# One state update for both heads in a chunked linear-attention recurrence, with third load buffers, an ordered weight preparation and scratch tensors split per 512 tokens

## Chip, cores and metric

The kernel runs on one core of one Trainium2 chip. The metric is device time in microseconds (us) of one execution; times before are the median of three runs, and the profile is one further execution.

## What is computed

One layer mixes 2048 tokens of width 1024 in float32. After a modulated RMS norm, one large projection gives the inputs of three mixers: two gated linear attentions (four heads each, key width 64, value width 128 in the first, "GLA", and 64 in the second, "HGRN") and a stick-breaking attention. Their outputs are normalised, gated, multiplied by an output matrix, added to the input and normalised again. The change touches the two gated linear attentions. Cut to what matters, they are, per chunk of 64 tokens:

```python
def step(state, inp):
    q_c, k_c, v_c, g_c = inp
    b_cum = jnp.cumsum(g_c, axis=2)
    ...
    scores = jnp.einsum('bhtd,bhsd,bhtsd->bhts', q_c, k_c, decay)
    o_c = (jnp.einsum('bhts,bhsv->bhtv', scores, v_c)
           + jnp.einsum('bhtd,bhdv->bhtv', q_c * jnp.exp(b_cum), state))
    b_last = b_cum[:, :, -1:, :]
    state = (jnp.exp(b_last[:, :, 0, :, None]) * state
             + jnp.einsum('bhsd,bhsv->bhdv', k_c * jnp.exp(b_last - b_cum), v_c))
    return state, o_c
```

## The kernel before, in words

The program has four stretches in time. First the norm, the modulation and the projections (to about 442 us in the trace), which also compute the decay sums of every chunk (`decay_sums`, L523 to L537) and store decays, queries, keys, values and gates in scratch tensors in device memory. Then the stick-breaking attention (`sb_stream`, to 854 us) with the rest of the projections beside it. Then the recurrence (to 1054 us), beside which the projection of the output gates fills TensorE. Last `phase2`: the outputs of 512 tokens are gathered with their gates, normalised and multiplied by the output matrix, four groups of 512 in turn.

The recurrence works on pairs of heads: two pairs of GLA, then two pairs of HGRN, and for each pair four tiles of 512 tokens (8 chunks), so 16 tiles, numbered 0 to 15 here. `gla_fast` (L879) loads for each tile decays `bc`, queries `qt` and keys `kt`, 128 x 512 each with one head in rows 0 to 63 and the other in rows 64 to 127 (L889 to L891, two buffers each), and `load_values` (L810) loads the values twice: as `Vn` in token order and, chunk by chunk, into `W[h]`.

`W[h]`, one tile per head, holds in 64 of its 128 rows the values of a chunk and in the other 64 the state before that chunk. `M[:, h]` matches it: masked scores in the rows of the values, decayed queries in the rows of the state (the queries' rows change sides for that, L911, one instruction per head). So one product of 128 rows per chunk and head gives the output `o` (L872). Because state rows lie on the other side from their keys, the decay of a chunk is also kept in a side-swapped copy `SX` (L533).

`gla_tail` (L830) goes in three steps: transposes of the keys (L838) and their copy `KTt` by ScalarE (L840); the products `U` of keys and values (L849) and the state updates on VectorE, one per chunk and head (L860):

```python
nc.vector.scalar_tensor_tensor(dst, W[h][orow, n, :], dec[orow, n:n + 1],
                               U[n % 2][orow, n // 2, :],
                               op0=ALU.mult, op1=ALU.add)
```

and the output products with their copies and stores (L872 to L877). `U`, `o`, the transposes and the scores `scp` (L919) have one buffer each in PSUM.

TensorE's order is written out by hand (the loop at L1062): scores and transposes of tile i, three steps of the gate projection (9 products of 512 columns), `U` of tile i, three more such steps, output products of tile i-1. The orders of VectorE, ScalarE, GpSimd and of the DMA queue on SyncE (SP) are set by a planner that simulates the program: an engine takes what its simulation has ready, and each engine then works strictly in that order. `scale_wo` (L1014) prepares one half of the output matrix in four steps from tile 8 of the program on: a load `wr` of 512 KB on SP, a product with the gate on GpSimd, a rounded copy `wh` and the rest `wl` on VectorE. Its `wr` shares two buffers with the gate projection's weight loads `wraw` (L140).

In scratch memory each of `s_gate`, `s_o` and the features is one tensor of 128 x 2048 (L58 to L67). `phase2` starts with tokens 0 to 511 (`prep(0)`): it loads `ot` from `s_o` and `gt` from `s_gate` on SP (L1125, L1129), multiplies them on VectorE and sums squares on TensorE. The gates of those tokens are computed in the second stretch, those of tokens 1024 to 2047 beside the recurrence.

Of the kernel before, what the change touches and what calls it, by code (L numbers as in the profile page):

```python
# [8 lines left out]
F32 = mybir.dt.float32  # L9
# [4 lines left out]
ALU = mybir.AluOpType  # L14
# [4 lines left out]
P = 128  # L19
T = 2048  # L20
# [22 lines left out]
def hybrid_mixer_kernel(ctx, tc, x, c, w_ada, b_ada, w_in, w2, bg, gnw, lbl, hnw,  # L43
# [10 lines left out]
    def act_tables(name):  # L54
# [39 lines left out]
    SE = const.tile([P, 4, T // GTF, 3 * NBF], F32, name="SE")  # L94
    SX = const.tile([P, 4, T // GTF, NBF], F32, name="SX")
    ada_b = const.tile([P, 16], F32, name="ada_b")
# [712 lines left out]

    def load_values(pools, pr, g, GT, Wn):  # L810
# [17 lines left out]
        return Vn, W, new_w() if g + 1 < T // GT else None  # L828

    def gla_tail(gr_, pp, pr, g, GT, M, kd, dec, Vn, W, Wn):  # L830
        gla = pr < 2
# [13 lines left out]
        for n in range(NB):  # L845
            rs = slice((n % 2) * 64, (n % 2) * 64 + 64)
            for h in range(2):
                orow = slice((1 - h) * 64, (1 - h) * 64 + 64)
                mm(U[n % 2][orow, n // 2, :], KTt[rs, n // 2, h * 64:(h + 1) * 64],  # L849
                   Vn[rs, n // 2, h * dv:(h + 1) * dv], start=True, stop=True)  # L850
        for n in range(NB):
            for h in range(2):
                orow = slice((1 - h) * 64, (1 - h) * 64 + 64)
                if n + 1 < NB:
                    dst = W[h][orow, n + 1, :]
                elif Wn is not None:
                    dst = Wn[h][orow, 0, :]
                else:
                    continue
                nc.vector.scalar_tensor_tensor(dst, W[h][orow, n, :], dec[orow, n:n + 1],  # L860
                                               U[n % 2][orow, n // 2, :],
                                               op0=ALU.mult, op1=ALU.add)
        yield


        no = 2 if gla else 1
        o = pp.tile([P, no, GT], F32, tag="o", name="o")
        for n in range(NB):
            ns = slice(n * CB, (n + 1) * CB)
            for h in range(2):  # L870
                dst = o[:, h, ns] if gla else o[h * 64:(h + 1) * 64, 0, ns]
                mm(dst, W[h][:, n, :], M[:, h, ns], start=True, stop=True)  # L872
        for a in range(no):
# [5 lines left out]
    def gla_fast(pairs, gp, gr_, pp, scp):  # L879

        for pr in pairs:
            gla = pr < 2
            j = pr % 2
            s = 1.0 / 16.0 if gla else 1.0
            Wn = None
            for g in range(T // GTF):
                tsl = slice(g * GTF, (g + 1) * GTF)
                bc, qt, kt = (gp.tile([P, GTF], F32, tag=t, name=t) for t in ("bc", "qt", "kt"))
                nc.sync.dma_start(bc, s_feat["da" if gla else "db"][j][:, tsl])  # L889
                nc.sync.dma_start(qt, s_feat["qa" if gla else "qb"][j][:, tsl])  # L890
                nc.sync.dma_start(kt, s_feat["ka" if gla else "kb"][j][:, tsl])  # L891
                Vn, W, Wn = load_values(gr_, pr, g, GTF, Wn)
# [16 lines left out]
                nc.gpsimd.tensor_tensor(v3(kd), v3(eN), per_chunk(2), op=ALU.mult)  # L909
                for h in range(2):  # L910
# [13 lines left out]
                for h in range(2):  # L924
                    hs = slice(h * 64, (h + 1) * 64)
                    nc.gpsimd.affine_select(v3(M[hs, h, :]), v3(S[hs]),
                                            pattern=[[0, NBF], [1, CB]], base=0,
                                            channel_multiplier=-1, compare_op=ALU.is_ge, fill=0.0)
                yield gla_tail(gr_, pp, pr, g, GTF, M, kd, SX[:, pr, g, :], Vn, W, Wn)

    def gla_exact(gp, pp):
# [4 lines left out]
        nc.sync.dma_start(mx, masks)  # L936
        M = gp.tile([P, 2, GT + NB], F32, name="M")
        nc.gpsimd.memset(M, 0.0)
        for pr in (2, 3, 0, 1):
            gla = pr < 2  # L940
            j = pr % 2
            s = 1.0 / 16.0 if gla else 1.0
            Wn = None
            for g in range(T // GT):
# [7 lines left out]
                nc.sync.dma_start(qt, s_feat["qa" if gla else "qb"][j][:, tsl])  # L952
                Vn, W, Wn = load_values(gp, pr, g, GT, Wn)
                if gla:
# [15 lines left out]
                def level(Xk, Xq, mi):  # L970
                    sc = pp.tile([P, NB, CB], F32, tag="sc", name="sc")
                    for n in range(NB):
                        for h in range(2):
                            hs = slice(h * 64, (h + 1) * 64)
                            ns = slice(n * CB, (n + 1) * CB)
                            mm(sc[hs, n, :], Xk[hs, ns], Xq[hs, ns], start=True, stop=True)
                    for h in range(2):
                        hs = slice(h * 64, (h + 1) * 64)
                        nc.vector.copy_predicated(
                            v3(M[hs, h, 0:GT]), mx[hs, mi:mi + 1, :].broadcast_to((64, NB, CB)), sc[hs])  # L980

# [21 lines left out]
                nc.vector.tensor_tensor(kt, kt, dd, op=ALU.mult)  # L1003
                for h in range(2):
                    nc.vector.tensor_copy(M[(1 - h) * 64:(2 - h) * 64, h, :], Qs[h * 64:(h + 1) * 64, :])
                dec = gp.tile([P, NB], F32, tag="dec", name="dec")
                for h in range(2):
                    orow = slice((1 - h) * 64, (2 - h) * 64)
                    nc.vector.tensor_copy(dec[orow], M[orow, h, GT:GT + NB])
                for _ in gla_tail(gp, pp, pr, g, GT, M, kt, dec, Vn, W, Wn):  # L1010
                    pass
# [21 lines left out]
    with ExitStack() as st:  # L1033
# [21 lines left out]
        with tc.manual_schedule(engines={ENG.PE}):  # L1055
# [6 lines left out]
            for i, tail in enumerate(gla_fast(GLA_ORDER, gp, gr_, pp, scp)):  # L1062
# [258 lines left out]
```

## Time and profile before

| | us |
|---|---|
| three runs, median | 1279.32 |
| three runs, lowest and highest | 1279.18, 1279.82 |
| the profiled execution's own time | 1281.43 |
| its span, first to last instruction | 1279.7 |

The profile's times are counted from the first instruction of the span. PE is TensorE (PEld its weight loads), DVE VectorE, ACT ScalarE, POOL GpSimd, SP the queue that issues most DMAs. A name such as `o<-M,W` says what is written from what. One float32 product appears as two instructions, so the 16 output products of a tile show as 32. "Idle before, and what ended it" names the instruction or DMA whose end released the waiting engine; "issue" there means that the profile shows no releaser. PEclk is the granted share of TensorE's full clock.

### The profile page before, as it was taken

The page shows a single profiled execution, that of the slowest core. Times are in us where ns is not written, and L with a number is a line of the kernel's source. Part 1 is how long each engine was busy: PE and PEld are TensorE (multiplying, and loading weights), DVE is VectorE, ACT ScalarE, POOL GpSimd, SP SyncE. Part 2 cuts the span into 40 slices and gives each one's busy share as a digit, 9 for nine tenths or more (in the row PEclk, how much of TensorE's full clock was granted, in tenths as well). Part 3 has the DMA queues.
Part 4 walks back from the last instruction along what each step waited for, and adds up shares of the span by engine and source line. Part 5 has one row for each costly group of instructions (what it writes and reads, how often), then busy time and mean ns, then how long its engine had stood idle before and what let it go on. Part 6 is the DMA issues. An engine that isn't in the chain of part 4 may idle for free.

```text
span 1279.7 us, 22082 instructions
## 1 busy us (share of the span) xinstructions
PE 1211.2 (95%) x8682; PEld 990.4 (77%) x8682; DVE 729.3 (57%) x1268; ACT 471.4 (37%) x860; POOL 160.5 (13%) x197
## 2 busy tenths in 40 slices
PE   7899999999999999999999999998988997999997
PEld 6678789999989877777777766776767774777775
DVE  4865424715243282544535598866886758665652
ACT  3377423424232242222323345543324333263521
POOL 3220000002111000000000001012442313010000
PEclk8999999999999999999999999998989897999999
DMA  9865442524222521332323413137887666464521
GB/s 263 247 230 181 151 124 79 157 87 132 79 78 101 156 69 50 89 89 80 86 71 98 114 55 83 35 104 239 241 238 197 199 192 216 131 215 137 200 83 52
DMA packets 177567, 173.75 MB, mean 136 GB/s; under 512 B 39625, under 2 KB 131882, under 8 KB 177454
## 3 DMA queue, kind: packets, MB, share of 16 engines
q1 hardware_dynamic: 144970, 128.70, 34.3%
q10 hardware_dynamic: 32484, 43.54, 9.8%
q8 instruction: 71, 1.16, 0.4%
q14 instruction: 42, 0.34, 0.1%
HBM read 113.47 MB, written 58.73 MB: 135 GB/s over the span
## 4 chain that ended last, share of the span: by engine, by line
PE 64%; DVE 8%; issue 7%; DMA 7%; ACT 2%; POOL 1%; SPq 0%; ACTq 0%; POOLq 0%; DVEq 0%
PE acc L154 6%; PE acc L156 6%; PE acc L155 6%; PE av L752 6%; PE acc L260 5%; PE pt L740 4%; PE y L1195 4%; PE y L1196 4%; PE y L1194 4%; PE acc L166 4%; PE acc L168 4%; PE acc L167 4%; PE zt L727 2%; PE zt L728 2%; DVE f L736 2%
## 5 line engine op out<-in xcount | busy, mean ns | idle before, releaser
L736 DVE TENSOR_TENSOR_SCAN f<-f 128x512 f32<-128x512 f32 (+3 forms) x160 | 169.7, 1090 | 29.3 <-POOL f L732 14.5
L154 PE MATMUL acc<-hTh,whi 128*128 128x512 f32 x400 | 159.0, 399 | 1.8 <-DVE stl L279 1.0
L155 PE MATMUL acc<-hTl,whi 128*128 128x512 f32 x400 | 157.0, 393 | 0.0
L156 PE MATMUL acc<-hTh,wlo 128*128 128x512 f32 x400 | 156.8, 393 | 0.0
L166 PE MATMUL acc<-whi,hTh 128*128 128x256 f32 (+1 forms) x512 | 146.2, 285 | 0.7 <-ACT stt L193 0.7
L168 PE MATMUL acc<-whi,hTl 128*128 128x256 f32 (+1 forms) x512 | 145.9, 285 | 0.0
L167 PE MATMUL acc<-wlo,hTh 128*128 128x256 f32 (+1 forms) x512 | 145.5, 284 | 0.0
L260 PE MATMUL acc<-hTh,whi 128*128 128x512 f32 x240 | 104.5, 435 | 1.9 <-ACT hTh L244 1.9
L260 PE MATMUL acc<-hTl,whi 128*128 128x512 f32 x240 | 98.5, 410 | 4.0 <-DVE hTl L250 3.8
L1196 PE MATMUL y<-wh,hTl 128*128 128x512 f32 x256 | 100.0, 395 | 2.4 <-DVE hTl L1162 2.4
L1195 PE MATMUL y<-wl,hTh 128*128 128x512 f32 x256 | 102.0, 398 | 0.0
L1194 PE MATMUL y<-wh,hTh 128*128 128x512 f32 x256 | 101.6, 399 | 0.0
L730 ACT ACTIVATE f<-zt 128x512 f32<-128x512 f32 (+3 forms) x160 | 82.2, 537 | 48.4 <-DVE f L736 21.4
L166 PEld LDWEIGHTS acc<-whi,hTh 128*128 128x128 f32 x512 | 97.8, 191 | 1.5 <-ACT stt L193 1.1
L260 PE MATMUL acc<-hTh,wlo 128*128 128x512 f32 x240 | 98.0, 408 | 0.0
L167 PEld LDWEIGHTS acc<-wlo,hTh 128*128 128x128 f32 x512 | 97.8, 191 | 0.2
L168 PEld LDWEIGHTS acc<-whi,hTl 128*128 128x128 f32 x512 | 97.7, 191 | 0.1
L154 PEld LDWEIGHTS acc<-hTh,whi 128*128 128x128 f32 x400 | 75.1, 188 | 19.6 <-issue 2.1
L752 PE MATMUL av<-PT,V 128*64 128x128 f32 x960 | 88.8, 280 | 0.7 <-DVE PT L745 0.7
L156 PEld LDWEIGHTS acc<-hTh,wlo 128*128 128x128 f32 x400 | 75.1, 188 | 16.8 <-issue 1.4
L740 PE MATMUL pt<-ident,f 128*128 128x128 f32 x544 | 86.7, 282 | 1.0 <-DVE f L736 0.7
L860 DVE SCALAR_TENSOR_TENSOR W<-W,SX,U 64x128 f32<-64x128 f32 (+1 forms) x248 | 77.7, 313 | 16.5 <-PE U L849 6.9
(206 smaller groups left out, 2086.9 us busy)
## 6 DMA issues: line engine op xcount, KB each, us to landing
wraw<-in_w_in_dram SPq DMA_DIRECT2D x36, 512.0 KB, 4.4
xt<-in_x_dram SPq DMA_DIRECT2D x16, 512.0 KB, 5.2
wa<-in_w_ada_dram SPq DMA_DIRECT2D x16, 512.0 KB, 6.3
Q<-s_qc SPq DMA_DIRECT2D x64, 128.0 KB, 3.2
ot<-s_o SPq DMA_DIRECT2D x32, 256.0 KB, 3.4
gt<-s_gate SPq DMA_DIRECT2D x32, 256.0 KB, 4.5
r<-in_x_dram SPq DMA_DIRECT2D x16, 512.0 KB, 5.6
out_dram<-r SPq DMA_DIRECT2D x15, 512.0 KB, 2.7
```

The lines of the kernel that those rows point to most:

```text
L154: mm(ps, hi[:, k, :], th[:, k, :], start=(k == 0), stop=False)
L155: mm(ps, hi[:, k, :], tl[:, k, :], start=False, stop=False)
L156: mm(ps, lo[:, k, :], th[:, k, :], start=False, stop=(k == KT - 1))
L166: mm(o, th[:, k, s], hi[:, k, 0:ncols], start=(k == 0), stop=False)
L167: mm(o, th[:, k, s], lo[:, k, 0:ncols], start=False, stop=False)
L168: mm(o, tl[:, k, s], hi[:, k, 0:ncols], start=False, stop=(k == KT - 1))
L260: mm(ps, a[:, k, :], b[:, k, :], start=(k == 0 and i == 0), stop=(k == KT - 1 and i == 2))
L736: nc.vector.tensor_tensor_scan(fr, fr, fr, carry[u], op0=ALU.mult, op1=ALU.bypass)
L752: last[0] = mm(av[u * 64:(u + 1) * 64, :], (Dd if diag else V)[J][:, b, :], PT[:, b, :], start=diag, stop=(J == 0 and b == 0))
L1194: mm(y, oh[:, k, us], wh, start=(k == 0), stop=False)
L1195: mm(y, oh[:, k, us], wl, start=False, stop=False)
L1196: mm(y, ol[:, k, us], wh, start=False, stop=(k == KT - 1))
```

## The change

Scores and queries get a tile of their own each (`Ms`, `Qd`), values and states too (`Vv`, `St`), all with the two heads in their own halves of the rows. A state update then covers both heads in one instruction of 128 rows, and decays are taken from `SE` directly, so `SX` goes. The output of a chunk and head becomes two products of 64 rows that accumulate in PSUM, values with scores and states with queries. `bc`, `qt`, `kt` get three buffers. The steps of `scale_wo` are called from tile 8 on with an order edge: their VectorE instructions come after the last state update of the tile. Feature, gate and output scratch tensors become four tensors of 512 tokens each. The code for large decays (`gla_exact`, not taken with these inputs) is changed to match.

```diff
-    s_feat = {n: [dram(f"s_{n}{j}", [P, T]) for j in range(2)]
+    class Chunks:
+        def __init__(self, name):
+            self.tiles = [dram(f"{name}_{n}", [P, 512]) for n in range(NCH)]
+        def __getitem__(self, at):
+            rows, cols = at
+            n = cols.start // 512
+            return self.tiles[n][rows, cols.start - n * 512:cols.stop - n * 512]
+    s_feat = {n: [Chunks(f"s_{n}{j}") for j in range(2)]
...
-    s_gate = [dram(f"s_gate{j}", [P, T]) for j in range(8)]
-    s_o = [dram(f"s_o{j}", [P, T]) for j in range(8)]
+    s_gate = [Chunks(f"s_gate{j}") for j in range(8)]
+    s_o = [Chunks(f"s_o{j}") for j in range(8)]
...
-        for h in range(2):
-            nc.vector.tensor_copy(SX[(1 - h) * 64:(2 - h) * 64, pr, n, :],
-                                  SE[h * 64:(h + 1) * 64, pr, n, NBF:2 * NBF])
...
-        def new_w():
-            return [pools.tile([P, NB, dv], F32, tag=f"W{h}", name=f"W{h}", bufs=2) for h in range(2)]
-        W = Wn if Wn is not None else new_w()
-        if Wn is None:
-            nc.gpsimd.memset(W[0][64:128, 0, :], 0.0)
-            nc.gpsimd.memset(W[1][0:64, 0, :], 0.0)
+        def new_s():
+            return pools.tile([P, NB, dv], F32, tag="St", name="St", bufs=2)
+        St = Sn
+        if St is None:
+            St = new_s()
+            nc.gpsimd.memset(St[:, 0, :], 0.0)
+        Vv = pools.tile([P, NB, dv], F32, tag="Vv", name="Vv", bufs=2)
         vr = vcols.rearrange("(n p) d -> p n d", p=CB)
-        nc.sync.dma_start(W[0][0:64], vr[:, :, 0:dv])
-        nc.sync.dma_start(W[1][64:128], vr[:, :, dv:2 * dv])
+        for h in range(2):
+            nc.sync.dma_start(Vv[h * 64:(h + 1) * 64], vr[:, :, h * dv:(h + 1) * dv])
...
-                orow = slice((1 - h) * 64, (1 - h) * 64 + 64)
-                mm(U[n % 2][orow, n // 2, :], KTt[rs, n // 2, h * 64:(h + 1) * 64],
+                mm(U[n % 2][h * 64:(h + 1) * 64, n // 2, :], KTt[rs, n // 2, h * 64:(h + 1) * 64],
                    Vn[rs, n // 2, h * dv:(h + 1) * dv], start=True, stop=True)
...
-                nc.vector.scalar_tensor_tensor(dst, W[h][orow, n, :], dec[orow, n:n + 1],
-                                               U[n % 2][orow, n // 2, :],
-                                               op0=ALU.mult, op1=ALU.add)
+            om[0] = nc.vector.scalar_tensor_tensor(dst, St[:, n, :], dec[:, n:n + 1], U[n % 2][:, n // 2, :],
+                                           op0=ALU.mult, op1=ALU.add)
...
-        o = pp.tile([P, no, GT], F32, tag="o", name="o")
+        o = pp.tile([P, no, 512], F32, tag="o", name="o")[:, :, 0:GT]
         for n in range(NB):
             ns = slice(n * CB, (n + 1) * CB)
-            for h in range(2):
-                dst = o[:, h, ns] if gla else o[h * 64:(h + 1) * 64, 0, ns]
-                mm(dst, W[h][:, n, :], M[:, h, ns], start=True, stop=True)
+            for x, y, first in ((Vv, Ms, True), (St, Qd, False)):
+                for h in range(2):
+                    hs = slice(h * 64, (h + 1) * 64)
+                    dst = o[:, h, ns] if gla else o[hs, 0, ns]
+                    mm(dst, x[hs, n, :], y[hs, ns], start=first, stop=not first)
...
-                bc, qt, kt = (gp.tile([P, GTF], F32, tag=t, name=t) for t in ("bc", "qt", "kt"))
+                bc, qt, kt = (gp.tile([P, GTF], F32, tag=t, name=t, bufs=3) for t in ("bc", "qt", "kt"))
...
-                M = gr_.tile([P, 2, GTF], F32, tag="M", name="M", bufs=3)
+                Ms, Qd = (gr_.tile([P, GTF], F32, tag=t, name=t, bufs=3) for t in ("Ms", "Qd"))
...
-                for h in range(2):
-                    nc.vector.tensor_tensor(v3(M[(1 - h) * 64:(2 - h) * 64, h, :]),
-                                            v3(eP[h * 64:(h + 1) * 64]),
-                                            per_chunk(0)[h * 64:(h + 1) * 64], op=ALU.mult)
+                nc.vector.tensor_tensor(v3(Qd), v3(eP), per_chunk(0), op=ALU.mult)
...
-                next(ws, None)
+                if i >= 8:
+                    with tc.issue_after(om[0].ins):
+                        next(ws, None)
```

## Rows read from the trace of the kernel before

**Rows 1.** Stretches: length, busy us (PE, PEld, DVE, ACT, POOL), PEclk, DMA share, GB/s.

```profile
298.00:442.00 144.00, 144.00 (x999) 135.08 (x998) 50.13 (x101) 40.69 (x81) 21.18 (x16) 1.00 0.34 107
...
862.80:1043.80 181.00, 158.65 (x2402) 130.78 (x2401) 134.15 (x326) 60.03 (x103) 56.38 (x58) 0.93 0.73 216
...
1053.60:1071.50 17.90, 9.25 (x24) 3.73 (x24) 13.41 (x21) 7.81 (x13) 1.81 (x1) 0.67 0.82 262
```

**Rows 2.** Timeline of PE in tiles 0 and 1, 4 and 5, 12 and 13.

```profile
862.77 1.09 PE L919 MATMUL scp<-eP,bc 64*32 64x64 f32 x64
...
869.76 1.09 PE L919 MATMUL scp<-eP,bc 64*32 64x64 f32 x64
...
910.86 1.09 PE L919 MATMUL scp<-eP,bc 64*32 64x64 f32 x64
...
914.53 1.10 PE L849 MATMUL U<-Vn,KTt 64*64 64x128 f32 x32
...
917.77 3.68 PE L872 MATMUL o<-M,W 128*128 128x64 f32 x32
921.38 1.09 PE L919 MATMUL scp<-eP,bc 64*32 64x64 f32 x64
...
1007.77 1.09 PE L919 MATMUL scp<-eP,kt 64*32 64x64 f32 x64
...
1014.35 1.15 PE L872 MATMUL o<-M,W 128*64 128x64 f32 x32
1015.43 1.09 PE L919 MATMUL scp<-eP,kt 64*32 64x64 f32 x64
```

**Rows 3.** Waits of PE in 862.8 to 1043.8 us: total, times, longest.

```profile
PE U L849 <- issue: 8.9, 4, 6.7
PE U L849 <- DVE W L860: 6.2, 7, 3.2
PE U L849 <- ACT KTt L840: 5.0, 3, 2.4
```

**Rows 4.** Timeline of all engines around the longest wait: start, length, idle before.

```profile
917.07 0.39 SPq L140 DMA_DIRECT2D wraw<-in_w_in_dram  x1
...
917.56 0.53 SPq L889 DMA_DIRECT2D bc<-s_da  x1
...
923.27 0.63 ACT L899 ACTIVATE eP<-bc 128x512 f32<-128x512 f32 x1 [9.21 <-DMA bc<-s_da]
...
931.38 1.10 DVE L860 SCALAR_TENSOR_TENSOR W<-W,SX,U 64x128 f32<-64x128 f32 x3
...
931.82 1.41 PE L849 MATMUL U<-Vn,KTt 64*64 64x128 f32 x12 [6.71 <-issue]
```

**Rows 5.** Groups of DVE by line and shape, 862.8 to 1043.8 us: busy, mean ns.

```profile
L860 DVE SCALAR_TENSOR_TENSOR W<-W,SX,U 64x128 f32<-64x128 f32 x124 | 43.0, 347 | 8.7 <-PE U L849 3.4 <-PE o L872 1.4
L860 DVE SCALAR_TENSOR_TENSOR W<-W,SX,U 64x64 f32<-64x64 f32 x124 | 34.7, 280 | 7.8 <-PE U L849 3.6 <-issue 0.3 <-PE scp L919 0.2
L911 DVE TENSOR_TENSOR M<-eP,SE 64x512 f32<-64x512 f32 x30 | 24.3, 808 | 0.7
```

**Rows 6.** Timeline: first load and first rounded copy of the output matrix.

```profile
895.07 0.38 SPq L1021 DMA_DIRECT2D wr<-in_w_out_dram  x1
...
905.80 0.69 DVE L1025 CAST wh<-wr 128x1024 fp32r<-128x1024 f32 x1
```

**Rows 7.** Group of the swapped decay copies, whole span.

```profile
L533 DVE COPY SX<-SE 64x8 f32<-64x8 f32 x32 | 5.3, 167 | 1.9 <-ACT SE L531 1.2
```

**Rows 8.** The chain of waits where the recurrence hands over: start, length, what.

```profile
1048.83 6.15 DMA s_gate<-st
...
1055.00 3.51 DMA gt<-s_gate
...
1061.26 3.70 DMA gt<-s_gate
...
1066.53 0.78 PE acc L1159
```

More of the change, by code (lines that the diff above doesn't have):

```diff
@@ L807, in hybrid_mixer_kernel, with load_values @@
     hpools[ORDER[2]].close()
-    def load_values(pools, pr, g, GT, Wn):
+    def load_values(pools, pr, g, GT, Sn):
         gla = pr < 2
@@ L817, in load_values, with gla_tail @@
         nc.sync.dma_start(Vn, vcols.rearrange("(b p) d -> p b d", p=P))
-        def new_w():
-            return [pools.tile([P, NB, dv], F32, tag=f"W{h}", name=f"W{h}", bufs=2) for h in range(2)]
-        W = Wn if Wn is not None else new_w()
-        if Wn is None:
-            nc.gpsimd.memset(W[0][64:128, 0, :], 0.0)
-            nc.gpsimd.memset(W[1][0:64, 0, :], 0.0)
-        vr = vcols.rearrange("(n p) d -> p n d", p=CB)
-        nc.sync.dma_start(W[0][0:64], vr[:, :, 0:dv])
-        nc.sync.dma_start(W[1][64:128], vr[:, :, dv:2 * dv])
-        return Vn, W, new_w() if g + 1 < T // GT else None
-    def gla_tail(gr_, pp, pr, g, GT, M, kd, dec, Vn, W, Wn):
+        def new_s():
[5 more added lines that the diff above has]
+        Vv = pools.tile([P, NB, dv], F32, tag="Vv", name="Vv", bufs=2)
+        vr = vcols.rearrange("(n p) d -> p n d", p=CB)
+        for h in range(2):
+            nc.sync.dma_start(Vv[h * 64:(h + 1) * 64], vr[:, :, h * dv:(h + 1) * dv])
+        return Vn, Vv, St, new_s() if g + 1 < T // GT else None
+    om = [None]
+    def gla_tail(gr_, pp, pr, g, GT, Ms, Qd, kd, dec, Vn, Vv, St, Sn):
         gla = pr < 2
@@ L847, in gla_tail @@
             for h in range(2):
-                orow = slice((1 - h) * 64, (1 - h) * 64 + 64)
-                mm(U[n % 2][orow, n // 2, :], KTt[rs, n // 2, h * 64:(h + 1) * 64],
+                mm(U[n % 2][h * 64:(h + 1) * 64, n // 2, :], KTt[rs, n // 2, h * 64:(h + 1) * 64],
                    Vn[rs, n // 2, h * dv:(h + 1) * dv], start=True, stop=True)
         for n in range(NB):
-            for h in range(2):
[L853 to L859, printed above, removed]
-                nc.vector.scalar_tensor_tensor(dst, W[h][orow, n, :], dec[orow, n:n + 1],
-                                               U[n % 2][orow, n // 2, :],
-                                               op0=ALU.mult, op1=ALU.add)
+            if n + 1 < NB:
+                dst = St[:, n + 1, :]
+            elif Sn is not None:
+                dst = Sn[:, 0, :]
+            else:
+                continue
+            om[0] = nc.vector.scalar_tensor_tensor(dst, St[:, n, :], dec[:, n:n + 1], U[n % 2][:, n // 2, :],
+                                           op0=ALU.mult, op1=ALU.add)
         yield
         no = 2 if gla else 1
-        o = pp.tile([P, no, GT], F32, tag="o", name="o")
+        o = pp.tile([P, no, 512], F32, tag="o", name="o")[:, :, 0:GT]
         for n in range(NB):
             ns = slice(n * CB, (n + 1) * CB)
-            for h in range(2):
-                dst = o[:, h, ns] if gla else o[h * 64:(h + 1) * 64, 0, ns]
-                mm(dst, W[h][:, n, :], M[:, h, ns], start=True, stop=True)
+            for x, y, first in ((Vv, Ms, True), (St, Qd, False)):
[3 more added lines that the diff above has]
+                    mm(dst, x[hs, n, :], y[hs, ns], start=first, stop=not first)
         for a in range(no):
@@ L884, in gla_fast @@
             s = 1.0 / 16.0 if gla else 1.0
-            Wn = None
+            Sn = None
             for g in range(T // GTF):
                 tsl = slice(g * GTF, (g + 1) * GTF)
-                bc, qt, kt = (gp.tile([P, GTF], F32, tag=t, name=t) for t in ("bc", "qt", "kt"))
+                bc, qt, kt = (gp.tile([P, GTF], F32, tag=t, name=t, bufs=3) for t in ("bc", "qt", "kt"))
                 nc.sync.dma_start(bc, s_feat["da" if gla else "db"][j][:, tsl])
@@ L925, in gla_fast @@
                     hs = slice(h * 64, (h + 1) * 64)
-                    nc.gpsimd.affine_select(v3(M[hs, h, :]), v3(S[hs]),
+                    nc.gpsimd.affine_select(v3(Ms[hs]), v3(S[hs]),
                                             pattern=[[0, NBF], [1, CB]], base=0,
                                             channel_multiplier=-1, compare_op=ALU.is_ge, fill=0.0)
-                yield gla_tail(gr_, pp, pr, g, GTF, M, kd, SX[:, pr, g, :], Vn, W, Wn)
+                yield gla_tail(gr_, pp, pr, g, GTF, Ms, Qd, kd, SE[:, pr, g, NBF:2 * NBF],
+                               Vn, Vv, St, Sn)
     def gla_exact(gp, pp):
@@ L936, in gla_exact @@
         nc.sync.dma_start(mx, masks)
-        M = gp.tile([P, 2, GT + NB], F32, name="M")
-        nc.gpsimd.memset(M, 0.0)
+        Ms = gp.tile([P, GT], F32, name="Ms")
+        nc.gpsimd.memset(Ms, 0.0)
         for pr in (2, 3, 0, 1):
@@ L942, in gla_exact @@
             s = 1.0 / 16.0 if gla else 1.0
-            Wn = None
+            Sn = None
             for g in range(T // GT):
@@ L976, in level @@
                             mm(sc[hs, n, :], Xk[hs, ns], Xq[hs, ns], start=True, stop=True)
[L977 to L980, printed above, removed]
+                    nc.vector.copy_predicated(
+                        v3(Ms), mx[:, mi:mi + 1, :].broadcast_to((P, NB, CB)), sc)
                 for lv in range(6):
@@ L1003, in gla_exact @@
                 nc.vector.tensor_tensor(kt, kt, dd, op=ALU.mult)
[L1004 to L1010, printed above, removed]
+                for _ in gla_tail(gp, pp, pr, g, GT, Ms, Qs, kt, Qs[:, GT:GT + NB], Vn, Vv, St, Sn):
                     pass
```

6 lines of the change are left out of this document (2 added, 4 removed).

## The prediction

> **What bounds the kernel now.** I read busy time by stretch first, then TensorE's timeline in undisturbed tiles, then its waits in the recurrence and the timeline of all engines around the longest of them. The reader should see that TensorE bounds every stretch, with one stretch that is not full. From 298 to 442 us it is busy 144.00 of 144.00 us; in the recurrence only 158.65 of 181.0 us, at a granted clock of 0.93 [rows 1]. So 22.4 us are idle, and the clock, which fell after the long waits, costs up to 0.07 x 181 = 12.7 us more: some 35 us. A second way to count gives the same. Undisturbed tiles show what TensorE needs: 10.52 us for a GLA tile (from 910.86 to 921.38), 7.66 us for an HGRN tile (1007.77 to 1015.43), 6.99 us for tile 0, which has no output products yet, and about 1.08 us for the last output products [rows 2]. Output products lag a tile, so 8 tiles have GLA length and 7 HGRN length: 6.99 + 84.16 + 53.62 + 1.08 = 145.9 us. The stretch takes 35.1 us more.
>
> The waits stand before U, on VectorE's updates and ScalarE's copy of the keys; the worst is 6.7 us with no releaser named [rows 3]. The timeline names it [rows 4]. SP issues the decays of tile 6 at 917.56, just behind a weight load at 917.07. ScalarE, which works strictly in order, sits 9.21 us until they land. VectorE's query product for tile 6 follows that exponential, and the last three state updates of tile 4 are queued behind it, at 931.38. U of tile 5 needs the bank they read and starts at 931.82. So work prepared two tiles ahead holds up work that is due, because its loads come late.
>
> **The change part by part.**
>
> *Third buffers.* With two, the decays of tile i+2 can only be fetched when the scores of tile i (tile 4 began at 910.86) have read theirs [rows 2, 4]. With three, a whole tile more, 7.7 to 10.5 us, lies between issue and need, more than the 5.7 us from 917.56 to 923.27, while the exponential's own output still has two buffers and so doesn't run further ahead. Bytes are unchanged; the mean DMA share is 0.73 [rows 1].
>
> *One update for both heads.* 248 updates become 124. Rows work in parallel: the 64 x 128 one takes 347 ns, the 64 x 64 one 280 ns [rows 5], the same length in columns at 128 rows, so VectorE loses about 77.7 / 2 = 39 us. The two query products of a tile become one: at the mean of 808 ns another 16 x 0.8 = 13 us. VectorE falls from 134 to about 82 of 181 us. None of this is on TensorE's path except through the waits; were a 128-row update twice as long, that relief would be nil.
>
> *What is late next.* Of the 35.1 us I leave 8: about 4 at the start, where tiles 0 to 2 load at once (a third buffer issues nothing sooner there; the wait for the key copy, 2.4 us at its longest, is of that kind [rows 3]), and 4 for the rest with the clock. Bounds: 2 and 18, half of what there is now.
>
> *Output products.* 16 products of 128 rows become 32 of 64 rows per tile, 64 instructions instead of 32. This is added work for the bounding engine. For GLA, 32 take 3.61 us (917.77 to 921.38), 113 ns each [rows 2]; they load 128 columns of weights and stream only 64, so the loads set the pace, and the new ones load 128 columns too. No row has 64-row products with 128 columns of weights. If the two heads, on different rows of the array, overlap fully, 64 x 113 / 2 = 3.6 us, no change; not at all, 7.2 us, +3.6. Nearest is the HGRN output, where two heads share the array by columns: 32 in 1.08 us, 34 ns each against half of 113, an overlap of 1.66. U, on four quarters, has 32 ns against 113, 3.5 of 4. I take 1.66: 4.36 us, +0.75 a tile, 6.0 in eight. For HGRN the new products use diagonal quarters; with 34 ns each 64 take 2.16 us, +1.08 a tile, 8.6 in eight. Bounds: +0.7 (28 ns, full overlap) and +2.5 (56 ns, none).
>
> Scores already do what the HGRN output will do: both heads, in different rows of the array, write into one bank, and 64 of them take about 1.05 us, 16 ns each [rows 2], less than half of U's. The Trainium skill, "TensorEngine Tiling (Array Packing)", section "Gotcha 1: PSUM Pressure", states that different row tiles cannot access the same PSUM bank simultaneously. By that rule the HGRN output would not overlap at all: the sum below would lose a further 11 us. The trace speaks against it.
>
> *Weight preparation.* Now it is done early: its first load goes out at 895.07 and its first copy is made at 905.80, in GLA tiles [rows 6]. After the change its 8 VectorE instructions follow the updates of tiles 8 to 11, a copy of 0.69 us and a remainder that I take as no more than twice that, about 2 us a tile, where VectorE needs some 4 to 5 us of 8.7; Its four products on GpSimd and its five loads on SP (one row of gates, four of 512 KB) get no edge, but a load's buffer is held until the copies are done. Behind them on VectorE stand the next tile's query product and the gate weights' remainder; behind a held buffer, SP's next gate-weight load and all that SP has after it. Cost taken: nothing, hidden by the slack of VectorE; without that cover a late weight load, 5 us, once or twice, inside the bound of 18.
>
> *Removed copies.* 32 x 167 ns = 5.3 us of VectorE [rows 7], in stretches where TensorE is full [rows 1]: nothing, 5.3 at most. Loads per tile stay six, the values' two included; one memset less per pair: nothing.
>
> *Scratch tensors per 512 tokens.* At the hand-over TensorE has 9.25 of 17.9 us [rows 1]. A store of gates at 1048.83, of other tokens, lands after 6.15 us, and only then, at 1055.00, goes a load of gates for tokens 0 to 511; the next, at 1061.26, waits for buffers behind it, and the first broadcast product comes at 1066.53 [rows 8]. With own tensors that load needs only a store long past. ScalarE's squares and TensorE's last gate products (to 1053.6) come next. I take 4 us of the 6.15; bounds 0 and 6. Elsewhere nothing.
>
> **The sum.** Recurrence: 145.9 + 6.0 + 8.6 + 8 = 168.5, 12.5 us less than 181.0; hand-over 4. From the profiled execution, 1281.43 (span 1279.7), that leaves 1264.9. That execution is 2.1 us above the median of the three runs, so in their terms **1263 us**. Measurements here tell about 0.2%, 2.6 us, from no change.
>
> **Rivals.**
> 1. *Near-full overlap.* The row halves overlap fully (GLA +0, HGRN 8 x 0.7 = 5.8), waits shrink to 2, the hand-over gives 6: 181 - 153.7 + 6 = 33 us less, 1246. U's 3.5 of 4 speaks for it, HGRN's 1.66 against.
> 2. *Late loads stay.* Extra buffers free the loads, but SP is one queue, and weight loads that wait for buffers stand ahead of them, as at 917.07. With 18 us of waits instead of 8: 2.5 + 4 = 6.5 less, 1273. If the third buffers change nothing at all, 22 us stay and it is about 1277, no change.
> 3. *The bank rule holds for HGRN.* 8 x 2.5 = 20 instead of 8.6: 1274. Against it, the scores' 16 ns.
> 4. *Slower: the row halves don't overlap.* GLA 8 x 3.6 = 29, HGRN 20, with waits of 4 left: 145.9 + 49 + 4 = 199, 18 more, less 4 at the hand-over: 1293. It decides from where the products add over 31 us (35 - 8 + 4), 1.9 us a tile. Against it, 34 ns and 32 ns on shared arrays; for it, that no row shows this shape.
>
> **Chances.** Forecast (1255 to 1270) 0.55, rival 1 0.13, rival 2 0.18 (of it faster 0.11, same 0.05, slower 0.02), rival 3 0.06, rival 4 0.08. Faster 0.55 + 0.13 + 0.11 + 0.06 = 0.85, same 0.05, slower 0.10. The range leaves out rival 4, the tail of rival 2 and the far end of rival 1: 1247 to 1275.
>
> **What would show it.** In the changed profile: TensorE's waits before U under 10 us in all, with no exponential waiting 9 us for decays; the clock of the recurrence back near 1; GLA output products at 4.0 to 4.7 us, HGRN at 1.8 to 2.5; 124 updates of 128 rows at 280 to 350 ns; the first broadcast product about 9 us after the last gate product instead of 13. GLA products at 6 us or more, or waits for loads above 15 us, would make the prediction wrong.

## The result, and the profile after

The changed kernel takes **1265.47 us** (median of six runs, 1262.56 to 1272.54) beside 1279.57 us for the kernel before in the same comparison (six runs, 1276.38 to 1283.29): a ratio of **0.9899, 95% interval 0.9880 to 0.9918**, 14.1 us less. 1263 was forecast, within 1247 to 1275. The profiled execution of after is the slowest of its six (1272.54 us, span 1270.4), so its trace shows somewhat more loss than the median.

Busy time by stretch, after: the recurrence and the hand-over (columns as in [rows 1]).

```profile
860.90:1036.50 175.60, 162.42 (x2914) 134.34 (x2913) 85.74 (x187) 58.68 (x103) 53.28 (x54) 0.95 0.74 226
...
1046.20:1063.30 17.10, 9.13 (x24) 3.64 (x24) 11.15 (x19) 7.37 (x12) 2.95 (x2) 0.68 0.79 253
```

Against [rows 1] the recurrence falls from 181.0 to 175.6 us, 5.4 less, though TensorE has more to do there. It is idle for 13.2 us instead of 22.4, the clock is 0.95 instead of 0.93, and VectorE's busy time falls from 134.2 to 85.7 us. The span as a whole is 9.3 us shorter; what is not in the recurrence is 1.9 us before it, 0.8 at the hand-over, 0.1 in the last gate products and 1.1 behind the hand-over.

TensorE's waits in that stretch, after; they answer to [rows 3].

```profile
PE U L858 <- ACT KTt L850: 12.4, 5, 4.2
PE o L880 <- issue: 0.7, 1, 0.7
```

The waits for VectorE's states (6.2 us) and the unnamed ones (8.9 us) are gone. Both were VectorE's: before each of the four unnamed ones the key copy had been done for 0.8 to 3.3 us, and U began as a state update of the tile before had read its bank, as in [rows 4]. Those for ScalarE's copy of the transposed keys have grown from 5.0 to 12.4 us. The timeline shows why (ScalarE, SP and TensorE of after, at the three places where a tile is long).

```profile
871.81 0.63 ACT L907 ACTIVATE eP<-bc 128x512 f32<-128x512 f32 x1 [3.20 <-DMA bc<-s_da]
...
875.89 2.08 PE L858 MATMUL U<-Vn,KTt 64*64 64x128 f32 x32 [4.22 <-ACT KTt L850]
...
981.20 0.73 ACT L915 ACTIVATE kt<-kt,loml 128x512 f32<-128x512 f32 x1 [7.76 <-DMA kt<-s_kb]
...
996.21 0.56 SPq L1019 DMA_DIRECT2D wr<-in_w_out_dram  x1
...
997.33 0.42 SPq L899 DMA_DIRECT2D kt<-s_kb  x1
...
1002.06 0.66 PE L848 MATMUL ptk<-ident,bc 128*128 128x128 f32 x4
...
1004.01 0.72 ACT L915 ACTIVATE kt<-kt,loml 128x512 f32<-128x512 f32 x1 [8.70 <-DMA kt<-s_kb]
...
1008.11 0.58 ACT L850 COPY KTt<-ptk 128x512 f32<-128x512 f32 x1
1008.74 1.13 PE L858 MATMUL U<-Vn,KTt 64*64 64x64 f32 x32 [3.96 <-ACT KTt L850]
```

Read the last six rows together. TensorE transposes the keys of tile 13 at 1002.06. ScalarE could copy them then, but it is 8.70 us into waiting for the keys of a later HGRN tile, whose load left SP at 997.33 behind a weight load. The copy comes at 1008.11 and U at 1008.74. From one tile's scores to the next, tile 13 takes 15.3 us where an undisturbed one takes 8.58; tile 11 takes 13.4 in the same way (the row of 981.20), and tile 1, where it is the decays of tile 2 that ScalarE waits for, 17.7 instead of 10.72. Other HGRN and GLA tiles are within 1 us of undisturbed.

TensorE's output products, after, first group of a GLA and of an HGRN tile with the scores that follow the last; they answer to the products in [rows 2].

```profile
957.20 0.44 PE L880 MATMUL o<-Ms,Vv 64*128 64x64 f32 x4
...
960.92 1.09 PE L924 MATMUL scp<-eP,kt 64*32 64x64 f32 x64
...
967.48 0.33 PE L880 MATMUL o<-Ms,Vv 64*64 64x64 f32 x4
...
969.49 1.09 PE L924 MATMUL scp<-eP,kt 64*32 64x64 f32 x64
```

64 GLA products take 3.72 us (957.20 to 960.92), 58 ns each, where 32 took 3.61. 64 HGRN products take 2.01 us, 31 ns each, where 32 took 1.08.

VectorE's groups by shape in the recurrence, after; they answer to [rows 5].

```profile
L867 DVE SCALAR_TENSOR_TENSOR St<-St,SE,U 128x128 f32<-128x128 f32 x62 | 21.5, 347 | 18.0 <-PE o L880 12.8 <-PE U L858 2.9
L867 DVE SCALAR_TENSOR_TENSOR St<-St,SE,U 128x64 f32<-128x64 f32 x62 | 17.4, 280 | 21.5 <-PE o L880 10.0 <-PE U L858 9.0
```

An update of 128 rows takes what one of 64 took, 347 and 280 ns, and there are half as many.

The hand-over, after: the chain of waits (start, length, what), which answers to [rows 8].

```profile
1037.12 3.19 DMA s_o<-oe
...
1041.71 5.75 DMA gt<-s_gate
```

The store of gates no longer stands in the chain. What releases SP's loads now is the last output store. The first broadcast product comes at 1058.33, 12.1 us after the last gate product, instead of 12.9.

### The profile page after: what moved, and what is told of

Its sections match the earlier page's. It is cut to its first block, busy times and chain, and to the rows that moved or that the text cites. A ratio compares the mean times of both kernels' runs of the same rounds, so it can differ in the third digit from the quotient of the medians.

```text
span 1270.4 us, 22877 instructions
## 1 busy us (share of the span) xinstructions
PE 1214.5 (96%) x9194; PEld 993.9 (78%) x9194; DVE 673.4 (53%) x1096; ACT 470.7 (37%) x860; POOL 155.2 (12%) x193
## 4 chain that ended last, share of the span: by engine, by line
PE 70%; issue 7%; DMA 5%; DVE 5%; ACT 1%; POOL 1%; SPq 1%; ACTq 0%; POOLq 0%; DVEq 0%
PE acc L163 6%; PE acc L165 6%; PE acc L164 6%; PE av L758 6%; PE acc L269 5%; PE pt L746 4%; PE y L1196 4%; PE y L1194 4%; PE y L1195 4%; PE acc L175 4%; PE acc L177 4%; PE acc L176 4%; PE o L880 3%; PE zt L733 2%; DVE f L742 2%
## 5 line engine op out<-in xcount | busy, mean ns | idle before, releaser
L164 PEld LDWEIGHTS acc<-hTl,whi 128*128 128x128 f32 x400 | 75.3, 188 | 15.1 <-issue 1.0
```

The costliest lines, as they stand in the source:

```text
L164: mm(ps, hi[:, k, :], tl[:, k, :], start=False, stop=False)
```

## The experiments

Each ratio is to the kernel before, run on the same chip in turn, with its 95% interval. "Excess" is the recurrence in the profiled execution less what its undisturbed tiles need: 145.9 us with the output products of before, 154.8 with those of after (7.0 + 8 x 10.72 + 7 x 8.58 + 2.0). Before has 35.1 us of it, after 20.8. It holds idle time and what a lower clock costs together: after has 13.2 us idle.

The theory from the prediction, A, is that the third buffers carry the gain; its rival, B, is that the halved updates do. The traces of after suggested theory C: what is left, and what the buffers only displace, is ScalarE's order, since the planner puts exponentials of later tiles, whose loads are late, ahead of the key copy that is due.

**Two buffers** (after, third buffers taken away):

```diff
-bc, qt, kt = (gp.tile([P, GTF], F32, tag=t, name=t, bufs=3) for t in ("bc", "qt", "kt"))
+bc, qt, kt = (gp.tile([P, GTF], F32, tag=t, name=t) for t in ("bc", "qt", "kt"))
```

> The changed kernel with two buffers for decays, queries and keys again. Theory A (the third buffers remove the waits before U): TensorE's waits in the recurrence rise from the 12 us of the changed kernel's profile to some 20, time about 1273 to 1277 us. Theory B (halving the state updates removes them, since VectorE no longer has the updates of tile i-1 queued behind late work of tile i+1): within 3 us of the changed kernel, 1262 to 1268.

Measured: 1.0006 (0.9990 to 1.0022), 1279.5 us, no gain left, and more lost than theory A had allowed for (1273 to 1277). ScalarE again waits mostly for decays, two of its waits over 10 us (its timeline):

```profile
901.52 0.63 ACT L907 ACTIVATE eP<-bc 128x512 f32<-128x512 f32 x1 [10.07 <-DMA bc<-s_da]
...
929.68 0.63 ACT L907 ACTIVATE eP<-bc 128x512 f32<-128x512 f32 x1 [10.08 <-DMA bc<-s_da]
```

The excess is 30.9 us; the 4.2 us less than before don't pay for the 8.9 us that the new products add. The halved updates do relieve VectorE: TensorE's waits for it fall from 15.1 us in before to 4.3 (two without a named releaser, read as above). But the waits for the key copy rise from 5.0 to 13.4 us. By themselves the halved updates are not what makes after faster.

**Third buffers alone** (the kernel before with `bufs=3` on that line, nothing else).

> The kernel before with only the third buffers. Theory A: most of the waits go and no output products are added, 1258 to 1268 us. Theory B: VectorE stays as full as it was and the waits stay, 1274 to 1280.

Measured: 0.9921 (0.9896 to 0.9946), 1269.1 us, most of the whole change, though 1 us above the range of theory A. The excess is 26.8 us. ScalarE's longest waits are no longer for decays but for the keys that HGRN exponentiates in place, of which the longest is:

```profile
933.16 0.72 ACT L907 ACTIVATE kt<-kt,loml 128x512 f32<-128x512 f32 x1 [9.16 <-DMA kt<-s_kb]
```

**Whole scratch tensors** (after; `Chunks` holds one tensor of T columns, `self.tile = dram(name, [P, T])`, and `__getitem__` returns `self.tile[at]`).

> The changed kernel with whole scratch tensors of 128 x 2048 again. The prediction's step says 4 us at the hand-over: about 1269 us. The changed kernel's profile shows that stretch only 0.8 us shorter, as loads now wait for a buffer that the last output store still reads: by that 1265 to 1268, no difference that can be told.

Measured: 0.9942 (0.9921 to 0.9964), 1270.7 us, 0.4% above after, with intervals that just miss each other. From the last gate product to the first broadcast product it takes 13.9 us instead of 12.1. So the tensors per 512 tokens are worth something, of which 1.8 us shows at the hand-over; the profiled executions (1271.56 and 1272.54 us) don't show where the rest would be. The hand-over alone is weak evidence: over all kernels here it takes 11.1 to 13.9 us with whole tensors and 10.3 to 12.1 with split ones.

**No edge on the weight preparation** (after):

```diff
-                if i >= 8:
-                    with tc.issue_after(om[0].ins):
-                        next(ws, None)
+                next(ws, None)
```

> The changed kernel with the output matrix's preparation free of its order edge. Prediction's step: the edge costs and gives nothing, 1263 to 1268 us. Rival: copies made early in the GLA tiles stand ahead of state updates and hold a weight buffer for shorter; if they hinder, 1269 to 1274, if the edge's held buffers hinder more (the load queue stands behind weight loads in the changed kernel's trace), 1257 to 1262.

Measured: 0.9953 (0.9935 to 0.9972), 1273.2 us, so the edge that was costed at nothing is worth 0.5%, and copies made early do hinder, as the rival has it. Tile 6 takes 22.0 us. Timeline of all engines there:

```profile
931.40 1.54 DVE L1024 TENSOR_TENSOR wl<-wr,wh 128x1024 fp32r<-128x1024 f32 x1
...
933.00 0.38 SPq L1019 DMA_DIRECT2D wr<-in_w_out_dram  x1
...
938.83 0.72 ACT L915 ACTIVATE kt<-kt,loml 128x512 f32<-128x512 f32 x1 [13.14 <-DMA kt<-s_kb]
...
939.82 1.52 DVE L1023 CAST wh<-wr 128x1024 fp32r<-128x1024 f32 x1 [5.68 <-POOL wr L1020]
...
941.98 0.58 ACT L850 COPY KTt<-ptk 128x512 f32<-128x512 f32 x1
942.65 2.71 DVE L867 SCALAR_TENSOR_TENSOR St<-St,SE,U 128x128 f32<-128x128 f32 x7
...
945.01 2.38 PE L858 MATMUL U<-Vn,KTt 64*64 64x128 f32 x32 [8.17 <-issue]
```

SP issues nothing between 923.4 and 933.00, when VectorE's `wl` frees the buffer for the next raw weights. Two engines sit behind that load. ScalarE waits 13.14 us for keys that left SP after it. VectorE waits 5.68 us to round these weights, and the eight due state updates of tile 5 stand behind that. The second is what ends last: the key copy of tile 6 is done at 942.56, but its U starts at 945.01, when the updates have read its bank. In the whole recurrence of this kernel TensorE waits before U 13.4 us for VectorE (2.3 named, 11.1 unnamed) and 4.5 for the key copy; in after it is nothing and 12.4. So the edge gives back what weight copies cost that stand ahead of due updates.

**Exponentials behind the key copy** (after, the direct trial of theory C; `kc[0]` is the copy `KTt<-ptk` of the preceding tile):

```diff
-                nc.scalar.activation(eP, bc, AF.Exp, scale=s)
+                with tc.issue_after(kc[0].ins) if kc[0] is not None else ExitStack():
+                    nc.scalar.activation(eP, bc, AF.Exp, scale=s)
+                    if gla:
+                        nc.scalar.activation(bc, bc, AF.Exp, scale=-s)
+                    else:
+                        nc.scalar.activation(kt, kt, AF.Exp, bias=loml[:, j:j + 1])
...
-                    nc.scalar.activation(eN, bc, AF.Exp, scale=-s)
...
-                    nc.scalar.activation(eN, kt, AF.Exp, bias=loml[:, j:j + 1])
```

> The changed kernel with one order edge more: ScalarE's exponentials of a tile come after its copy of the keys of the tile before. Theory C (the 12 us of waits that remain stand before U because ScalarE waits, in order, for loads of work two tiles ahead, which the third buffers let the planner put there): the waits behind the copy of the keys go, 1253 to 1261 us. Rival: the exponentials then come late for the scores and TensorE waits there instead, 1264 to 1275.

Measured: 0.9837 (0.9818 to 0.9855), 1258.2 us. The excess falls to 5.4 us, tile 1 from 17.7 to 11.4. TensorE's waits in the recurrence:

```profile
PE ptk L849 <- POOL bc L921: 1.6, 1, 1.6
PE U L859 <- issue: 0.9, 1, 0.9
PE U L859 <- ACT kt L913: 0.9, 1, 0.9
PE o L881 <- issue: 0.7, 1, 0.7
PE U L859 <- ACT KTt L851: 0.5, 1, 0.5
```

12.4 us of waits for the key copy have become 0.5, with the same loads and buffers in the code. Theory C is shown for the waits that after has left.

**The same with two buffers.**

> Two buffers for decays, queries and keys, and the order edge on the exponentials. If the order in which ScalarE takes the work is what matters and the third buffers are not needed: 1253 to 1261 us, as with the edge and three buffers. If the loads also need the third buffers' earlier issue: 1263 to 1272.

Measured: 0.9816 (0.9802 to 0.9829), 1255.2 us, excess 6.0 us. Once the order is right the third buffers bring nothing. So what they gave without the edge was that ScalarE's wrong order hurt less.

**Head by head** (after, the two loops over the output products exchanged, so that neighbours use the same rows of the array):

```diff
-            for x, y, first in ((Vv, Ms, True), (St, Qd, False)):
-                for h in range(2):
+            for h in range(2):
+                for x, y, first in ((Vv, Ms, True), (St, Qd, False)):
```

> The changed kernel with the two output products of one head next to each other, so that neighbours use the same rows of the array. If the overlap of the two row halves is what makes 64 instructions take 3.7 us in a GLA tile, neighbours in the same rows overlap less: up to 7.2 us a GLA tile and 3.5 us an HGRN tile, 1285 to 1305 us. If TensorE overlaps them whatever their order, 1263 to 1268.

Measured: 0.9899 (0.9876 to 0.9922), 1266.6 us, the same as after. GLA products of one tile and the next scores:

```profile
900.31 0.45 PE L880 MATMUL o<-Ms,Vv 64*128 64x64 f32 x4
...
904.08 1.09 PE L924 MATMUL scp<-eP,bc 64*32 64x64 f32 x64
```

3.77 us instead of 3.72: what was expected of the neighbours' order is wrong. The half time of a 64-row product doesn't hang on which product stands next to it; whether the row halves overlap, or a product of 64 rows takes half as long by itself, no run here tells. This kernel's profiled execution (1265.42 us) is near its median; its waits for the key copy, 10.0 us in five, stand at the same tiles, so the reading of after doesn't come from an odd run.

**The edge on the kernel before** (two buffers, 248 updates, old products, whole scratch tensors).

> The kernel before, whole, with one edge only: the ScalarE exponentials of a tile behind the copy of the preceding tile's transposed keys. Two buffers, 248 state updates of 64 rows, output products over 128 rows, whole scratch tensors. Theory C (ScalarE's order is the price, and nothing else of the change is needed for it): the recurrence falls from 181 us to about 148 to 154, the clean tiles of the kernel before, and the ratio is 0.975 to 0.983, at or below that of the version with the edge and all of the change. Rival (with the order right VectorE is the next bound, because 134 us of its work must fit the same stretch in order, and so the halved updates earn their place): the waits of TensorE for VectorE's state stay at 6 us and more, the recurrence takes 160 us or more, and the ratio is 0.985 to 0.992.

Measured: 0.9869 (0.9847 to 0.9891). One edge of order does at least as much as the whole change. But theory C's second half, that nothing else is needed, fails: the recurrence takes 165.5 us, not 148 to 154. From the second HGRN tile's scores to the last output products it takes 58.1 us, 3.4 over undisturbed (busy time by stretch, this kernel):

```profile
968.50:1026.60 58.10, 55.75 (x1084) 44.45 (x1083) 49.95 (x145) 24.12 (x42) 17.62 (x23) 1.00 0.73 216
```

GLA tiles 4 and 6, where the weights are prepared here, take 17.1 and 18.5 us. VectorE's states are named for 0.8 us of TensorE's waits only, but the largest have no name (waits of PE, then the timeline of tile 4):

```profile
PE U L851 <- issue: 9.9, 3, 4.9
```

```profile
904.28 0.59 ACT L842 COPY KTt<-ptk 128x512 f32<-128x512 f32 x1
...
906.94 0.69 DVE L1030 CAST wh<-wr 128x1024 fp32r<-128x1024 f32 x1
...
908.42 1.23 DVE L1031 TENSOR_TENSOR wl<-wr,wh 128x1024 fp32r<-128x1024 f32 x1
909.68 0.34 DVE L862 SCALAR_TENSOR_TENSOR W<-W,SX,U 64x128 f32<-64x128 f32 x1
...
910.12 1.99 PE L851 MATMUL U<-Vn,KTt 64*64 64x128 f32 x32 [4.93 <-issue]
```

The key copy is done at 904.87. U starts at 910.12, right behind a state update of the tile before, which stands on VectorE behind `wh` and `wl`; tile 6 is the same. So TensorE waits for VectorE for 10.7 us in all, and the rival holds in its three signs (6 us and more, 160 us or more, 0.985 to 0.992): with ScalarE's order right, VectorE's is next. The key copy is waited for 1.2 us. With the rest of the change as well, but two buffers, it was 0.9816: clear of this kernel's interval, so the rest is worth some 0.5% once ScalarE's order is right.

**The edge, the weights' edge and the scratch tensors on the kernel before.**

> The kernel before with the exponentials' edge, the weight preparation's edge (behind the last state update issued) and the scratch tensors per 512 tokens, but two buffers, 248 updates of 64 rows and the old output products. If the halved updates and the row-half output products give a net loss (8 HGRN tiles at +0.93 us are 7.4 us of TensorE), this is the fastest so far: 0.3 to 0.9% below the kernel with the exponentials' edge alone, 0.972 to 0.979. If VectorE's 248 updates bind once the order is right, it stays above 0.9816, the ratio of the version with the edge, two buffers and the rest of the change.

Measured: 0.9839 (0.9825 to 0.9854), 1260.19 us. Now TensorE's waits before U for VectorE are 3.1 us (1.1 named, 2.0 unnamed), every GLA tile but the second (11.9) is within 0.7 us of undisturbed, and the HGRN tiles lose instead (the same stretch of this kernel):

```profile
955.20:1025.40 70.20, 59.82 (x1084) 46.49 (x1083) 61.84 (x153) 25.04 (x43) 25.00 (x25) 0.95 0.73 214
```

VectorE is busy 61.84 of 70.20 us there. Against the edge with two buffers and the rest of the change (0.9816) this kernel differs by the old updates and products, with the query products and decay copies that belong to them: with the order right the new ones may be worth some 0.2%, but the intervals overlap, so it isn't shown.

**Outputs staged elsewhere** (two buffers and the edge; the output tile's memory is no longer reused by the tail):

```diff
-            oe = gr_.tile([P, GT], F32, tag="oe", name="oe")
+            oe = stg.tile([P, 512], F32, tag="st", name="oe")[:, 0:GT]
```

> The version with the exponentials' edge and two buffers, with the eight output tiles of the recurrence taken from the staging pool that stays open, so that no load of the tail waits for an output store through reused memory. Theory (the loads of the tail wait on SP for the last output stores, whose source memory they reuse): the stretch from the last gate product to the first broadcast product falls from 10.9 us to 6 to 9, and the ratio from 0.9816 to 0.978 to 0.980. Rival (other memory of the recurrence, or the loads' own latency, sets the stretch): it stays within 1 us of 10.9 and the ratio within 0.002 of 0.9816; the gates' evictions now share their three buffers with the outputs, which could cost up to 2 us.

Measured: 0.9825 (0.9807 to 0.9844), hand-over 10.5 us instead of 10.9: the rival. In the kernel that it is built on (two buffers and the edge) the loads were already early enough. VectorE's timeline in that one, from the last gate product to the broadcast:

```profile
1030.17 0.15 DVE L1095 TENSOR_REDUCE fs<-pf 1x1 f32<-1x2 f32 x1 [2.54 <-PE pf L1093]
...
1034.15 0.75 DVE L1145 SCALAR_TENSOR_TENSOR ot<-ot,gnc,gt 128x512 f32<-128x512 f32 x1 [0.43 <-DMA gt<-s_gate]
...
1038.97 0.69 DVE L1148 TENSOR_TENSOR ot<-ot,gt 128x512 f32<-128x512 f32 x1 [0.89 <-DMA gt<-s_gate]
...
1040.05 0.68 DVE L1158 TENSOR_TENSOR rh<-rs,rh 8x512 fp32r<-8x512 f32 x1
```

From 1030.17 to 1040.73 VectorE waits 1.3 us for gates; the rest is its own work in order, begun only when the flag `fs`, which needs the last products of TensorE, has gone through. In the staged kernel VectorE takes its first product at 1029.83, ahead of the flag (1032.23), and its later waits for gates come to 1.8 us; the stretch is no shorter than 10.5 us.

**Mixed** (two buffers and the edge; GLA pairs as in after, HGRN pairs with the states, updates and products of before; the diff is cut to the output products):

```diff
+            if old:
+                for h in range(2):
+                    mm(o[h * 64:(h + 1) * 64, 0, ns], St[h][:, n, :], Ms[:, h, ns], start=True, stop=True)
+                continue
             for x, y, first in ((Vv, Ms, True), (St, Qd, False)):
```

> The version with the exponentials' edge and two buffers, but the HGRN pairs in the form of the kernel before (states in swapped rows, 64-row updates, output products over 128 rows) and the GLA pairs in the form of the change; the weights of the output projection still in the HGRN tiles. If TensorE's time sets the HGRN tiles, eight of them lose 0.93 us each and the ratio is 0.975 to 0.977. Rival (VectorE sets them, since there it has the second update, the two halves of the scaled queries and the weight preparation): the eight HGRN tiles take 66 to 70 us as in the kernel before with the edge and the rest, and the ratio is 0.979 to 0.983, that of the version with the change throughout.

Measured: 0.9832 (0.9815 to 0.9849), the rival, if just past its range. All full GLA tiles are at 10.7 us, and from the second HGRN tile to the end of the recurrence it takes 70.7 us with VectorE busy for 62.19. (That stretch, of seven tiles, is what the expectation calls eight HGRN tiles.) Busy time there, and TensorE's longest waits:

```profile
953.00:1023.70 70.70, 61.70 (x1085) 48.83 (x1083) 62.19 (x153) 25.15 (x43) 25.72 (x25) 0.90 0.75 211
```

```profile
PE U L877 <- issue: 6.7, 3, 3.1
```

All three of these waits stand in this stretch (967.58, 980.05 and 1000.25); each ends as a state update of the tile before ends, some 3 us after the key copy.

**Mixed, with the weights from the fourth GLA tile on** (`if i == 3:` and `if i >= 3:` in place of 8).

> The same mixed version with the weights of the output projection prepared from the fourth GLA tile on, where VectorE is idle for over half of the time, instead of in the HGRN tiles. If VectorE is what the HGRN tiles of the mixed version wait for, they fall to about 58 to 62 us, as in the kernel before with the exponentials' edge alone, the GLA tiles stay at 10.7 us each, and the ratio is 0.972 to 0.976, the fastest of all. If instead the loads on SP set the tiles (the raw weights block the queue wherever they are put), one or two GLA tiles grow by 3 to 8 us and the ratio is 0.976 to 0.983.

Measured: **0.9795 (0.9778 to 0.9812)**, 1254.69 us, the lowest ratio of all, though its interval overlaps that of the edge with two buffers. Busy time in the HGRN part, this kernel:

```profile
959.10:1017.30 58.20, 55.82 (x1085) 44.52 (x1083) 50.63 (x147) 24.12 (x42) 17.35 (x23) 1.00 0.73 218
```

The HGRN part falls from 70.7 to 58.2 us by moving the weights alone, and VectorE's busy time in it from 62.19 to 50.63, as expected if VectorE's load held them. But the GLA tiles don't all stay at 10.7 us, and the ratio is that of the other side, the loads on SP: one GLA tile grows to 16.2 us, where TensorE waits 3.9 us for a key copy (timeline of that tile):

```profile
898.51 1.22 DVE L1069 TENSOR_TENSOR wl<-wr,wh 128x1024 fp32r<-128x1024 f32 x1
899.77 0.38 SPq L150 DMA_DIRECT2D wraw<-in_w_in_dram  x1
...
903.92 1.04 ACT L151 CAST whi<-wraw 128x1024 fp32r<-128x1024 f32 x1 [8.42 <-DMA wraw<-in_w_in_dram]
...
906.88 0.59 ACT L868 COPY KTt<-ptk 128x512 f32<-128x512 f32 x1
```

ScalarE sits 8.42 us in the rounding of gate weights, with the key copy behind it. Their load leaves SP at 899.77, as `wl` ends and frees the buffer that the two kinds of weights share. Both sides of the expectation hold, each at its place.

## Why the prediction was right, and where not

The time is 2.5 us from the forecast, and that is in part luck: terms missed in opposite directions, and in the profiled execution, the slowest of six, 9.3 us came of 16.5. Of its own signs the waits before U (12.4 us, not under 10), the clock (0.95), the GLA products (3.72 us, not 4.0 to 4.7) and the broadcast product (12.1 us, not 9) failed; the HGRN products, the updates and the decays' waits came as said. By its own steps, profiled against profiled:

- **Waits left in the recurrence, with the clock: 8 us forecast, 20.8 found** (13.2 idle, the rest at a lower clock). This is the step that failed, and not by the slow execution alone: the exchanged version, profiled near its median, has 17.4. Its ground was that "the exponential's own output still has two buffers and so doesn't run further ahead". That is true of the product `eP`, not of HGRN's second exponential, which is written over the keys themselves: with a third buffer the planner puts it a tile further ahead, and ScalarE waits for its load with the due copy behind it (7.76 and 8.70 us). The 4 us at the start were put down to three tiles loading at once; tile 1 loses 7.0, and the edge on the exponentials takes it to 0.6, with two buffers to nothing, so that was order too. The sign was right: the third buffers alone give 0.9921. Rival 2's "22 us stay" if the third buffers change nothing counted the idle time and left the clock out; without them the excess is 30.9 and the gain nil.
- **Output products: +14.6 us forecast (6.0 + 8.6), +8.9 found.** For GLA the time is that of full overlap of the row halves (58 ns, half of 113), so +0.1 us of products, +0.2 a tile, instead of +0.75; the row chosen as nearest, the HGRN output's 1.66, was the wrong neighbour, and U's 3.5 of 4 the right one. HGRN's +0.93 is close to the +1.08.
- **Rival 3, the bank rule.** 64 HGRN products, two heads in different rows of the array and one bank, take 31 ns each, not 56 or more. The Trainium skill, "TensorEngine Tiling (Array Packing)", section "Gotcha 1: PSUM Pressure", states that different row tiles cannot access the same PSUM bank simultaneously; this trace shows no such cost.
- **Updates: right in size** (347 and 280 ns at 128 rows, 38.8 us less on VectorE), with 85.7 us of busy time where 82 were forecast. That they bring something only through the waits was right as well: with two buffers and no edge the waits move from VectorE to the key copy, and nothing is left net.
- **Weight preparation: 0 forecast, about 0.5% found** (0.9899 with the edge, 0.9953 without). The prediction named the blocked queue, "behind a held buffer, SP's next gate-weight load and all that SP has after it", as a risk of the new place; the old place pays it, and more by the due state updates that stand on VectorE behind the weight copies.
- **Hand-over: 4 us forecast, 0.8 found.** The 6.15 us of the store [rows 8] were taken as if nothing else were nearly as late. The last output store and VectorE's own work were: with all loads early the stretch still takes 10.5 us, so some 2.4 of 12.9 were to be had.
- **Removed copies: nothing forecast, 5.3 us at most; 1.9 us less stand before the recurrence.** In the four kernels with all the copies it begins at 860.9 to 862.8 us, in the eight without at 858.8 to 861.3: one profile each, so a gain of some 2 us is likely but not shown.

Together for the recurrence: 12.8 us more lost to waits and the lower clock, and 5.7 less work than forecast, 7.1 over; 3.2 over at the hand-over; 3.1 under elsewhere. That gives 9.3 us less than before in the profiled executions, where 16.5 were forecast.

## What to carry to other kernels

Before more buffers are given to work prepared ahead, look at which in-order engine issues it, and what that engine has due behind it: one edge of order (0.9869 alone) did as much as buffers, new layout, scratch tensors and the weights' edge together (0.9899). When that wait is gone, look again: the next one was VectorE's, with weight copies ahead of due updates. And look past the named releaser: the largest waits here had none, and the timeline gave it. A buffer limits how far a planner runs ahead only for what is written into it; a step that works in place follows its input's buffers. Work without a deadline, like a weight's preparation, goes where its engine idles, and behind what is due there: moving it from the HGRN to the GLA tiles gave 12.5 us in the first, though it cost one GLA tile 5.5.

## What the runs showed that was not expected

- Products with 64 rows and 128 columns of weights take 58 ns each, two heads on the two row halves, against 113 ns with 128 rows; exchanging the neighbours so that equal rows follow each other changes nothing (3.77 and 3.72 us for 64).
- The clock followed the order too: granted 1.00 over the 160 us of the recurrence in both versions of after with the edge, where TensorE waits for nothing longer than 1.6 us, and 0.95 in after, which is up to 0.05 x 175.6 = 8.8 us beside the 12.4 of waits.
